# A two-layer streaming encoder step: more PSUM banks for the factors and the first heads, the queries' norm beside the heads, and another order of the final norm

## The chip, the core and the metric

The kernel runs on one core of a Trainium2 chip. The time is the device time of one execution in microseconds (us), as the median of several runs. The engines of the core are named as in the profile: PE (TensorE, the matrix products), DVE (VectorE), ACT (ScalarE), POOL (GpSimd) and SP (SyncE, which here only issues DMAs). Each engine works through its own list of instructions in order; an instruction that must wait for another engine or a DMA holds up all that stands behind it on its engine.

## What is computed

One step of a hybrid encoder for two groups of requests that share the weights: 512 tokens of a new stream and 64 of a running one, 576 columns in all, of width 1024, through two layers. Cut to what matters here:

```python
def layer(x, ...):
    x = swiglu_half(x, ffn1_norm, ffn1_w_gate, ffn1_w_up, ffn1_w_down)
    y, c_kv, k_r, wkv, shift = token_mixer(rmsnorm(x, mix_norm), ...)
    x = x + y
    x = mem_attend(x, mk, mv, lp)
    x = swiglu_half(x, ffn2_norm, ...)

def token_mixer(h, ...):
    c_q, c_kv, k_r, p_b = split(h @ w_in)                    # latents and RWKV rows
    q = (rmsnorm(c_q, q_norm) @ w_uq).reshape(b, t, 8, 96)   # 8 heads
    c_kv = rmsnorm(c_kv, kv_norm); k_r = rope(k_r, pos)
    y_a = latent attention of q over c_kv and k_r, past ones too
    kk = k * k_k * rsqrt(sum(kk * kk) + 1e-12)
    S = S * w + (S @ -kk) (kk * a) + v k;  y = S @ r         # per token, 8 heads of 64
    return concat(y_a, y_b) @ w_out, ...

y = rmsnorm(x, final_norm)                                   # after both layers
```

`rmsnorm(x, g)` is `x * rsqrt(mean(x * x) + 1e-6) * g`.

## The kernel before

The activations lie transposed in SBUF: features on the 128 partitions, the T = 576 columns as two halves of HT = 288 (`hs`). Every fp32 product is made of three products of rounded parts and remainders (lines 316 to 318, one call of `mm3`). `split` (L248 on ACT, L249 on DVE) makes the rounded part, for instance `kfh`, and the remainder, `kfl`. PSUM has eight banks, one bank per tile of a tag here.

The mixer of a layer has two stages. In the preparation two banks belong to tag `g`, four to `mm` (two tiles of two banks), one each to `sp` and `fx`. `STEPS` is the written order of its steps. `key`, `gate` and `rest` make projections in `mm`. `factors(p4)`, for four pairs of heads, spreads the keys' norm (L777, tag `sp`) and makes the lower triangles `ad` of each of the nine chunks of 64 tokens (L792 on PE, L793 on DVE, tag `fx`). They go to DRAM. `inverse(g)`, g = 0 and 1, each for two of these pairs, gathers the diagonal blocks of 16 (L814), inverts them by fifteen pairs of small DVE instructions (L818, L819), copies the result transposed (`td`, L820) and sends both to DRAM by eight DMAs (L824). `bonus` multiplies with L843 and L844. `keys` and `queries` make the latents: four of 128 features, each half 24 products into `g`, evicted by DVE L857. `rotated` makes the rotated key (`krh`, `krl`). The last step, `normed`, makes the root of the queries' norm: L361 sums the squares into an `mm` tile, and `rsqrt` (Ln, Exp, Square on ACT, L301; L350 and L351 on DVE) makes `rq`.

Then the scopes are closed and the banks given to the next stage, with tags `sc`, `tp`, `po`, `pp` of one bank and `sm` of two; `g` stays. `attention()` is a generator: for each of four pairs of heads (`pr_`) it makes values (`vp`, `vs`), keys (`kf`, `kc`) and queries (`qf`, multiplied by `rq`), each product in the next tile of `bank()`. For `pr_` 0 that goes through `g`, `g`, `sm`, `sm`, later through `g` alone. Beside it `memory(l)` makes the keys and values of the memory (`g<-x` products), and the chain goes through the nine chunks: `prepare(c)` loads `ck`, `bk` and the inverse blocks `DI` (L1090 to L1093), multiplies `bk` with `ck` (L1100, `pp`), and goes on with `batch` (L1076), the first reader of `DI`.

The final norm (`final`) is part of the last feed-forward stage. There the last four x tiles are written by halves (`some`, the add is DVE L550). `tail(a)` squares the eight x tiles of half a (ACT L1447), adds them (DVE L1449), sums over partitions (PE L1450, L1453) and takes the root. Then four outputs of two tiles each follow: two by ACT L1459 and DVE L1460, two by DVE L1463, and eight DMAs in all. `tail(0)` is called after the second x add of half 1, `tail(1)` at the end.

A scheduler sets the order of the instructions on each engine, by a timeline of its own. Who writes into a bank that another tile held before waits for that tile's last reader.

Of the kernel before, what the change touches and what calls it, by code (L numbers as in the profile page):

```python
# [11 lines left out]
AF = mybir.ActivationFunctionType  # L12
# [38 lines left out]
for _n, _c in (("ones", 128), ("eps", 4), ("id", 128), ("bd", 128), ("cen", 128), ("sel8", 32), ("sel", 128), ("mA", 256), ("mD", 64),  # L51
# [12 lines left out]
STEPS = (("decays",), ("gates",), ("key", 0), ("gate", 0), ("gate", 1), ("key", 1), ("gate", 2), ("gate", 3), ("norms", 0),  # L64
         ("key", 2), ("factors", 0), ("key", 3), ("factors", 1), ("norms", 2), ("rest", 0), ("inverse", 0), ("factors", 2),
         ("bonus", 0), ("factors", 3), ("rest", 1), ("inverse", 1), ("rest", 2), ("bonus", 1), ("rest", 3), ("bonus", 2),
         ("keys",), ("bonus", 3), ("queries",), ("rotated",), ("normed",))


def columns(op, p4=None):  # L70
# [62 lines left out]
def build(tc, I, O):  # L133
# [267 lines left out]
    def ffn(l, which, V, aside=iter(()), final=None, given=()):  # L401
# [136 lines left out]
        def last_outputs(g, acts, by_halves=None):  # L538

            w2 = [take(0 if by_halves else 2) for _ in range(2)]  # L540
            w4 = []

            def some(i, s):
                p = ps1("b")[:, 0:HT]
                for f in range(4):
                    mm3(p, cols(w4[i], f), [t[:, s] for t in acts[f]], f == 0, False)
                for f in range(2):
                    end = mm3(p, cols(w2[i // 2], i % 2 * 2 + f), [t[:, s] for t in acts[4 + f]], False, f == 1)
                o = x[4 * g + i][:, s]
                DVE.scalar_tensor_tensor(out=o, in0=p, scalar=0.5, in1=o, op0=ALU.mult, op1=ALU.add)  # L550
                return end

            for i in range(4):
                w4.append(take(0 if by_halves else (2, 2, 2, 1)[i]))
                for s in hs[0:1] if by_halves else hs:
                    some(i, s)
            if by_halves:
                for i in range(4):
                    end = some(i, hs[1])
                    if i == 1:  # L560
                        by_halves(end)


        def plain(act, ps=None, parts=(0, 1)):
# [102 lines left out]
        if final is None:  # L667
            last_outputs(1, acts)
        else:
            half_done, done = final()  # L670
            last_outputs(1, acts, half_done)
            done()
        ps.close()
        sc.close()

    def mixer(l, V, xn):
# [85 lines left out]
        def factors(p4):  # L762
# [8 lines left out]
            POOL.tensor_copy(wend[:, p4], wt[:, CH - 1::CH])  # L771
            wts.append(wt)
            kk = st([128, T], "kk")
            for s in hs:
                p = ps1("sp")
                rks[p4 // 2].to(p[:, 0:HT], p4 % 2, s)
                DVE.scalar_tensor_tensor(out=kk[:, s], in0=xk[:, s], scalar=V("kk", p4), in1=p[:, 0:HT], op0=ALU.mult, op1=ALU.mult)  # L777
            at, bk = st([128, NC, 64], "aa"), st([128, NC, 128], "big")
# [7 lines left out]

            ad = st([128, NC, 64], "ad")
            for c0, n in ((0, 5), (5, 4)):
                pa = ps1("fx")
                for c in range(c0, c0 + n):  # L790
                    for e in range(2):
                        PE.matmul(pa[half(e), (c - c0) * 64:(c - c0) * 64 + 64], bk[half(e), c, half(1)], at[half(e), c], start=True, stop=True)  # L792
                DVE.tensor_tensor(out=ad[:, c0:c0 + n], in0=pa[:, 0:64 * n].rearrange("p (c t) -> p c t", c=n),  # L793
                                  in1=C("mD").unsqueeze(1).to_broadcast([128, n, 64]), op=ALU.mult)
# [13 lines left out]
        def inverse(g):  # L808

            NP = 8 * NC  # L810
            adg, pr, tt, td = (st([128, 2, 16, 16], "x")[0:NP] for _ in range(4))
            for i in range(2):
                for e in range(2):
                    SP.dma_start(adg[36 * e:36 * e + 36, i], diagonal(ads[2 * g + i][e]))  # L814
                DVE.tensor_copy(tt[:, i], C("e16")[0:NP].rearrange("p (j s) -> p j s", j=16))
            for t in range(1, 16):
                q = pr[:, :, 0:t, 0:t]
                DVE.tensor_tensor(out=q, in0=tt[:, :, 0:t, 0:t], in1=adg[:, :, 0:t, t].unsqueeze(2).to_broadcast([NP, 2, t, t]), op=ALU.mult)  # L818
                DVE.tensor_reduce(out=tt[:, :, 0:t, t], in_=q, axis=AX.X, op=ALU.add)  # L819
            DVE.tensor_copy(td, tt.rearrange("p i j s -> p i s j"))  # L820
            for n, t_ in enumerate((td, tt)):
                for e in range(2):
                    for i in range(2):
                        SP.dma_start(diagonal(dinv[e, n, 2 * g + i]), t_[36 * e:36 * e + 36, i])  # L824
# [47 lines left out]
        for op, *n in STEPS:  # L872
# [12 lines left out]
            elif op == "queries":  # L885
                cq = [latent(nrm.rstd()) for j in range(2)]
                sqs = [squares(t) for t in cq]
                DVE.tensor_tensor(out=sqs[0], in0=sqs[0], in1=sqs[1], op=ALU.add)

                qn = []  # L890
                for j in range(2):
# [4 lines left out]
            elif op == "rotated":  # L896
                pr4 = full(C("sel"), [kr])
                krh, krl = st([128, T], "krh", F32R), st([128, T], "krl", F32R)
                split(pv(pr4), (halves(krh), halves(krl)), "kr")
                ACT.activation(out=halves(kr)[0:32], in_=pv(pr4)[0:32], func=AF.Copy)  # L900
                SP.dma_start(O["krope"][l], kr[0:32])
                cc2 = st([128, 2, PAST], "nacc")
                SP.dma_start(cc2[:, 0], I["cckv"][l])
                SP.dma_start(cc2[:, 1], I["ckrope"][l])
                cch, ccl = split(cc2, None, "cc")
                ccv = (cch[:, 0], ccl[:, 0])
            elif op == "normed":
                rq = rsqrt(pv(full(ones, sqs[0:1])), 1.0 / 256, EPS, st([128, T], "rq"), st([128, T], "rs"), halves)
        SP.dma_start(O["shift"][l], shout)
        lat.close()  # L910
        xn.close()
# [12 lines left out]
        def attention():  # L924
# [2 lines left out]

            def bank():

                tags_ = ("g", "g", "sm", "sm") if pr_ == 0 else ("g",)  # L930
                turn[0] += 1
                return ps1(tags_[(turn[0] - 1) % len(tags_)])
            kch, kcl = st([128, 2, PAST], "kch", F32R), st([128, 2, PAST], "kcl", F32R)
            for pr_ in range(4):
# [34 lines left out]
                mm3(p[:, 0:PAST], wp_[0], ccv, True, True)  # L969
                for e in range(2):  # L970
                    split(p[half(e), 0:PAST], (kch[half(e), e], kcl[half(e), e]), "kc")
                for e in range(2):
                    nr, rr = half(e), half(1 - e)
                    qf = st([128, T], "qf")
# [462 lines left out]

    def final():

        r, sq = st([128, T], "rstd"), st([128, T], "rs")  # L1440
        y = [st([128, 2, HT], "s") for _ in range(8)]

        def tail(a, prior=None):
            ss, s = ps1("b")[:, 0:HT], hs[a]
            qs = [st([128, 2, HT], "s")[:, 0] for _ in range(8)]
            for k in range(8):
# [4 lines left out]
            if prior is not None:  # L1451
                after(i, prior)
            PE.matmul(ss, ones, qs[7], start=False, stop=True)  # L1453
            rsqrt(ss, 1.0 / D, EPS, r[:, s], sq[:, s])
            for j in range(4):
                t = y[2 * j + a]
                if j < 2:
                    for i in range(2):
                        ACT.activation(out=t[:, i], in_=x[2 * j + i][:, s], func=AF.Copy, scale=V("fin", 2 * j + i))  # L1459
                    DVE.tensor_tensor(out=t, in0=t, in1=r[:, s].unsqueeze(1).to_broadcast([128, 2, HT]), op=ALU.mult)  # L1460
                else:
                    for i in range(2):
                        DVE.scalar_tensor_tensor(out=t[:, i], in0=x[2 * j + i][:, s], scalar=V("fin", 2 * j + i), in1=r[:, s], op0=ALU.mult, op1=ALU.mult)  # L1463
                SP.dma_start(O["y"][2 * j:2 * j + 2, :, s].rearrange("k p t -> p k t"), t)
        return [lambda prior=None, a=a: tail(a, prior) for a in range(2)]

    xn = open_xn()
    load_x()
# [104 lines left out]
```

## Time and profile before

| | us |
|---|---|
| median of three runs | 2796.2 |
| lowest, highest | 2794.36, 2797.31 |
| the profiled execution | 2796.16 |
| its span | 2794.4 |
| PE busy | 2740.6 |
| DVE busy | 2102.2 |
| ACT busy | 1352.5 |

The span runs from the first to the last event of the trace; some 1.8 us of the execution lie outside it. The busy time of PE counts its products also where the granted clock is halved, and so slow work counts as more. Layer 1 runs through the same program as layer 0; its hand-over from preparation to chain stands 1381.35 us later in the trace.

### The profile page before, as it was taken

How to read it: one execution, taken by the hardware profiler on the slowest of the kernel's cores; microseconds unless marked ns; L12 is line 12 of the kernel's file. 1: busy time of each engine (PE TensorE's matmuls, PEld its weight loads, DVE VectorE, ACT ScalarE, POOL GpSimd, SP SyncE). 2: the span in 40 equal slices, each digit the busy share in tenths (PEclk: the TensorE clock that was granted, in tenths of full speed). 3: DMA queues.
4: the chain of work that ended last, by engine and by line, in shares of the span. 5: the costliest groups of instructions: out<-in, count | busy, mean ns of one | idle time of the engine just before them, and what ended most of it. 6: DMA issues, size and time to landing. Idle time of an engine off the chain costs nothing.

```text
span 2794.4 us, 55844 instructions
## 1 busy us (share of the span) xinstructions
PE 2740.6 (98%) x22290; PEld 2639.7 (94%) x22290; DVE 2102.2 (75%) x4317; ACT 1352.5 (48%) x2787; POOL 86.3 (3%) x189
## 2 busy tenths in 40 slices
PE   9999999999999999999999999998999999999997
PEld 9999999888889899999999999998888899999997
DVE  8988866876677578777788778678666766887785
ACT  5554455455545544444554444544555445454443
POOL 0000001101000000000000000011010000000000
PEclk9999999989999999999999999998999999999998
DMA  5333334643333222222323222347433232232221
GB/s 194 113 115 116 104 129 117 177 117 96 106 104 121 69 92 83 91 91 91 93 75 105 91 91 91 111 117 178 116 106 118 84 111 72 84 99 91 91 84 65
DMA packets 187893, 293.47 MB, mean 105 GB/s; under 512 B 87130, under 2 KB 113370, under 8 KB 187458
## 3 DMA queue, kind: packets, MB, share of 16 engines
q1 hardware_dynamic: 185330, 285.72, 33.0%
q0 software_dynamic: 2304, 4.20, 0.6%
q8 instruction: 175, 2.87, 0.4%
q14 instruction: 84, 0.69, 0.1%
HBM read 250.63 MB, written 41.63 MB: 105 GB/s over the span
## 4 chain that ended last, share of the span: by engine, by line
PE 94%; DVE 3%; ACT 2%; DMA 1%; issue 0%; SPq 0%; DVEq 0%; ACTq 0%
PE b L318 19%; PE b L316 19%; PE b L317 18%; PE mm L316 4%; PE mm L318 4%; PE mm L317 4%; PE g L316 3%; PE g L317 3%; PE g L318 3%; PE sm L1076 2%; PE sc L316 2%; PE pp L1076 1%; PE pp L1100 1%; PE sc L317 1%; PE sc L318 1%; PE tp L1029 1%
## 5 line engine op out<-in xcount | busy, mean ns | idle before, releaser
L248 ACT ACTIVATE whi<-wraw 128x512 fp32r<-128x512 f32 (+1 forms) x497 | 308.1, 624 | 509.0 <-PE b L317 246.1
L249 DVE TENSOR_TENSOR wlo<-wraw,whi 128x512 fp32r<-128x512 f32 (+1 forms) x497 | 336.6, 680 | 114.4 <-ACT whi L248 97.5
L318 PE MATMUL b<-s,wlo 128*128 128x288 f32 x1376 | 405.4, 296 | 0.0
L317 PE MATMUL b<-s,whi 128*128 128x288 f32 x1376 | 403.0, 294 | 0.0
L316 PE MATMUL b<-s,whi 128*128 128x288 f32 x1376 | 399.4, 295 | 0.0
L316 PE MATMUL b<-xnh,whi 128*128 128x288 f32 x1128 | 332.4, 296 | 1.5 <-ACT whi L248 1.5
L317 PE MATMUL b<-xnl,whi 128*128 128x288 f32 x1128 | 332.2, 295 | 0.7 <-DVE xnl L372 0.7
L318 PE MATMUL b<-xnh,wlo 128*128 128x288 f32 x1128 | 331.3, 295 | 0.0
L317 PEld LDWEIGHTS b<-s,whi 128*128 128x128 f32 x1376 | 258.9, 188 | 0.1
L318 PEld LDWEIGHTS b<-s,wlo 128*128 128x128 f32 x1376 | 258.3, 188 | 0.0
L316 PEld LDWEIGHTS b<-s,whi 128*128 128x128 f32 x1376 | 256.4, 188 | 0.0
L318 PE MATMUL b<-s,sl 128*128 128x288 f32 x768 | 225.4, 295 | 0.0
L316 PE MATMUL b<-s,sh 128*128 128x288 f32 x768 | 224.2, 296 | 0.0
L317 PE MATMUL b<-s,sh 128*128 128x288 f32 x768 | 223.9, 292 | 0.0
L316 PEld LDWEIGHTS b<-xnh,whi 128*128 128x128 f32 x1128 | 211.9, 188 | 2.5 <-ACT whi L248 2.2
L317 PEld LDWEIGHTS b<-xnl,whi 128*128 128x128 f32 x1128 | 212.3, 188 | 1.3 <-DVE xnl L372 1.1
L318 PEld LDWEIGHTS b<-xnh,wlo 128*128 128x128 f32 x1128 | 211.7, 188 | 0.0
L318 PE MATMUL mm<-xnh,wlo 128*128 128x288 f32 x688 | 204.0, 297 | 0.0
L529 DVE SCALAR_TENSOR_TENSOR x<-b,x 128x288 f32<-128x288 f32 x320 | 140.2, 457 | 84.7 <-PE b L318 84.6
L316 PE MATMUL mm<-xnh,whi 128*128 128x288 f32 x688 | 203.8, 297 | 0.0
L317 PE MATMUL mm<-xnl,whi 128*128 128x288 f32 x688 | 203.4, 296 | 0.0
L248 ACT ACTIVATE whi<-S 128x512 fp32r<-128x512 f32 x172 | 108.5, 631 | 156.2 <-PE b L317 153.4
(511 smaller groups left out, 7351.8 us busy)
## 6 DMA issues: line engine op xcount, KB each, us to landing
wraw<-in_wgu SPq DMA_DIRECT2D x131, 512.0 KB
wraw<-in_wds SPq DMA_DIRECT2D x50, 512.0 KB
sraw<-in_wgu SPq DMA_DIRECT2D x45, 512.0 KB
wraw<-in_win SPq DMA_DIRECT2D x36, 512.0 KB
wraw<-in_wd SPq DMA_DIRECT2D x19, 512.0 KB
wraw<-in_wmk SPq DMA_DIRECT2D x16, 512.0 KB
wraw<-in_wmv SPq DMA_DIRECT2D x16, 512.0 KB
wraw<-in_wout SPq DMA_DIRECT2D x32, 256.0 KB
```

The costliest lines, as they stand in the source:

```text
L248: ACT.activation(out=h, in_=src, func=AF.Copy)
L249: by.tensor_tensor(out=lo, in0=src, in1=h.bitcast(F32), op=ALU.subtract)
L316: PE.matmul(out, wh, ah, start=first, stop=False, **kw)
L317: PE.matmul(out, wh, al, start=False, stop=False, **kw)
L318: return PE.matmul(out, wl, ah, start=False, stop=last, **kw)
L529: DVE.scalar_tensor_tensor(out=o, in0=p, scalar=0.5, in1=o, op0=ALU.mult, op1=ALU.add)
L1029: PE.transpose(pT[0:n, c0:c0 + nq], pe_[e][0:nq, kt * 128:kt * 128 + n], ident[0:nq, 0:nq])
L1076: PE.matmul(o, *f(p4, e), start=(n == 0 and p4 == 0), stop=(n == len(terms) - 1), skip_group_check=True)
L1100: i = PE.matmul(p[:, p4], bk[half(e), p4], ck[half(e), p4, 0:128], start=True, stop=True)
```

## The change

- The step `normed` goes. The queries' sums of squares are added into the tile `rq`; in `attention`, for the first pair of heads and behind the keys of the past (`kc`), two products by halves sum them over partitions in the banks `po` and `tp`, and `rsqrt` works on each half.
- `bank()` takes turns over `g`, `g`, `sm`, `sm`, `sc` for the first pair of heads.
- `factors`: the two halves of L777's spread lie in `sp` and `fx`; the two parts of L792 lie in `g` (two banks).
- `inverse`: the four DMAs of `tt` are issued ahead of the transposed copy `td`, then the copy and its four.
- The final norm: ACT's Square of the root writes a tile `s` of its own instead of `rs`, whose old readers are the last matmuls; the first half's sums come after the first x add of half 1 instead of the second. Of the first half's outputs the two that are made by DVE alone (j > 1) stand behind the last x add, and the second half's sums are written ahead of the outputs.

```diff
-         ("keys",), ("bonus", 3), ("queries",), ("rotated",), ("normed",))
+         ("keys",), ("bonus", 3), ("queries",), ("rotated",))
...
-                DVE.scalar_tensor_tensor(out=o, in0=p, scalar=0.5, in1=o, op0=ALU.mult, op1=ALU.add)
-                return end
+                return end, DVE.scalar_tensor_tensor(out=o, in0=p, scalar=0.5, in1=o, op0=ALU.mult, op1=ALU.add)
...
-                    end = some(i, hs[1])
-                    if i == 1:
+                    end, added = some(i, hs[1])
+                    if i == 0:
                         by_halves(end)
+                return added
...
-            last_outputs(1, acts, half_done)
-            done()
+            done(last_outputs(1, acts, half_done))
...
-            for s in hs:
-                p = ps1("sp")
+            for s, tag in zip(hs, ("sp", "fx")):
+                p = ps1(tag)
                 rks[p4 // 2].to(p[:, 0:HT], p4 % 2, s)
...
             for c0, n in ((0, 5), (5, 4)):
-                pa = ps1("fx")
+                pa = ps1("g")
...
-            DVE.tensor_copy(td, tt.rearrange("p i j s -> p i s j"))
-            for n, t_ in enumerate((td, tt)):
+            for n, t_ in ((1, tt), (0, td)):
+                if n == 0:
+                    DVE.tensor_copy(td, tt.rearrange("p i j s -> p i s j"))
...
-                DVE.tensor_tensor(out=sqs[0], in0=sqs[0], in1=sqs[1], op=ALU.add)
+                rq = st([128, T], "rq")
+                DVE.tensor_tensor(out=rq, in0=sqs[0], in1=sqs[1], op=ALU.add)
...
-            elif op == "normed":
-                rq = rsqrt(pv(full(ones, sqs[0:1])), 1.0 / 256, EPS, st([128, T], "rq"), st([128, T], "rs"), halves)
...
-                tags_ = ("g", "g", "sm", "sm") if pr_ == 0 else ("g",)
+                tags_ = ("g", "g", "sm", "sm", "sc") if pr_ == 0 else ("g",)
...
+                if pr_ == 0:
+
+                    pq, sq = [ps1(t)[:, 0:HT] for t in ("po", "tp")], st([128, T], "ya")
+                    for s, p in zip(hs, pq):
+                        PE.matmul(p, ones, rq[:, s], start=True, stop=True)
+                    for s, p in zip(hs, pq):
+                        rsqrt(p, 1.0 / 256, EPS, rq[:, s], sq[:, s])
...
-        r, sq = st([128, T], "rstd"), st([128, T], "rs")
+        r, sq = st([128, T], "rstd"), st([128, 2, HT], "s")
...
+        def scaled(a, j, prior=None):
...
+        def first_half(prior):
+            root(0, sums(0, prior))
+
+        def rest(last):
+            ss = sums(1)
+            for j in range(4):
+                scaled(0, j, last if j > 1 else None)
+            root(1, ss)
+            for j in range(4):
+                scaled(1, j)
+        return first_half, rest
```

The scheduler moves instructions in three places: the preparation and the hand-over of each layer, up to the chain's third chunk or so, and the end. In the lists below one row is one instruction (or as many as stand behind the x) with its line, result and operands; line numbers of the changed kernel are up to six higher in the mixer.

PE, layer 0, the first pair of heads. Before, the last product of the values, then the queries' norm in `mm`, the values and keys of the past in `sm`, the keys in `g`:

```order
L318 MATMUL g<-whi,ckvl 128x256
L361 MATMUL mm<-nsq,cst 128x288 x2
L316 MATMUL sm<-whi,cch 128x256
L317 MATMUL sm<-wlo,cch 128x256
L318 MATMUL sm<-whi,ccl 128x256
```

After, from the keys in `sc` on, with the queries' norm in `po` and `tp` and the first query of the heads behind it:

```order
L316 MATMUL sc<-ckvh,whi 128x288
L317 MATMUL sc<-ckvl,whi 128x288
L318 MATMUL sc<-ckvh,wlo 128x288
L975 MATMUL po<-rq,cst 128x288
L975 MATMUL tp<-rq,cst 128x288
L316 MATMUL sm<-qnh,whi 128x288
L317 MATMUL sm<-qnl,whi 128x288
L318 MATMUL sm<-qnh,wlo 128x288
```

The products of the norm moved behind all of the values and the first half of the keys. Further up, the last factors now stand ahead of the latents, whose eight halves of 24 products follow each other with two L843 between; further down, 51 products of the memory's keys and values stand between the heads' first products and the first reader of `DI`, where there were 26.

DVE, layer 0, the end of the second inverse (its last two steps are 72x2x14x14 and 72x2x15x15, its copy is `x<-x 72x512`). Before, it runs beside the first heads:

```order
L249 TENSOR_TENSOR kfl<-g,kfh 64x288
L249 TENSOR_TENSOR kcl<-sm,kch 64x256
L819 TENSOR_REDUCE x<-x 72x2x14
L818 TENSOR_TENSOR x<-x 72x2x15x15
L819 TENSOR_REDUCE x<-x 72x2x15
L981 TENSOR_TENSOR qf<-g,cst 64x288
L820 COPY x<-x 72x512
L982 TENSOR_TENSOR qf<-qf,rq 128x576
```

After, with the last latent's eviction (L857), the rotated key's remainder, the copy, the queries' sums of squares and their root:

```order
L817 TENSOR_TENSOR x<-x 72x2x15x15
L857 TENSOR_TENSOR lx<-g,rstd 128x288
L818 TENSOR_REDUCE x<-x 72x2x15
L249 TENSOR_TENSOR wlo<-wraw,whi 128x512
L249 TENSOR_TENSOR krl<-mm,krh 128x576
L821 COPY x<-x 72x512
L889 TENSOR_TENSOR rq<-nsq 128x576
L895 SCALAR_TENSOR_TENSOR qnl<-lx,narrow,qnh 128x576
L249 TENSOR_TENSOR wlo<-wraw,whi 128x512
L350 SCALAR_TENSOR_TENSOR ya<-po,ya 128x288
L350 SCALAR_TENSOR_TENSOR ya<-tp,ya 128x288
L351 SCALAR_TENSOR_TENSOR rq<-ya,rq 128x288 x2
```

The second inverse moved ahead, from beside the heads to between the latents' evictions, and its copy stands ahead of all that the heads read from DVE. ACT's root by halves stands ahead of its copies `vph` and `vs`, and the rotated keys (`kfh`, `kfl`, four entries) behind these.

DVE at the end of the program. Before, with the first half's root and outputs (L1460, L1463) ahead of the last x add (L550):

```order
L550 SCALAR_TENSOR_TENSOR x<-b,x 128x288 x4
L350 SCALAR_TENSOR_TENSOR rs<-b,rs 128x288
L351 SCALAR_TENSOR_TENSOR rstd<-rs,rstd 128x288
L1460 TENSOR_TENSOR s<-s,rstd 128x576 x2
L1463 SCALAR_TENSOR_TENSOR s<-x,narrow,rstd 128x288 x4
L550 SCALAR_TENSOR_TENSOR x<-b,x 128x288
L1449 TENSOR_TENSOR s<-s 128x288 x6
L350 SCALAR_TENSOR_TENSOR rs<-b,rs 128x288
```

After, where L1455 adds the squares and L1472 and L1470 make the outputs:

```order
L550 SCALAR_TENSOR_TENSOR x<-b,x 128x288 x3
L350 SCALAR_TENSOR_TENSOR s<-b,s 128x288
L351 SCALAR_TENSOR_TENSOR rstd<-s,rstd 128x288
L1455 TENSOR_TENSOR s<-s 128x288 x2
L550 SCALAR_TENSOR_TENSOR x<-b,x 128x288
L1455 TENSOR_TENSOR s<-s 128x288 x4
L550 SCALAR_TENSOR_TENSOR x<-b,x 128x288
L1472 SCALAR_TENSOR_TENSOR s<-x,narrow,rstd 128x288 x4
L1470 TENSOR_TENSOR s<-s,rstd 128x576 x2
L350 SCALAR_TENSOR_TENSOR s<-b,s 128x288
```

The six instructions of the first half's outputs moved behind the last x add, and the sums of the second half's squares between the adds. On ACT eight scaled copies (L1469) of both halves stand between the last Square of x and the Ln of the second half, where four stood.

## Rows read from the trace of the kernel before

**Rows 1.** The page, part 1: busy us (share of the span) xinstructions.
```profile
PE 2740.6 (98%) x22290; PEld 2639.7 (94%) x22290; DVE 2102.2 (75%) x4317; ACT 1352.5 (48%) x2787; POOL 86.3 (3%) x189
```

**Rows 2.** Waits of PE over the span: total us, times, longest us.
```profile
PE b L1450 <- DVE s L1449: 6.6, 1, 6.6
PE g L316 <- DVE kfl L249: 6.5, 3, 3.1
PE sm L316 <- DVE rs L350: 6.1, 2, 3.1
PE pp L1076 <- DMA DI<-d: 4.5, 2, 3.1
```

**Rows 3.** Timeline of PE, hand-over of layer 0: start, us, instruction [idle before].
```profile
547.57 0.78 PE L843 MATMUL fx<-xs,cst 128*128 128x320 f32 x2 [0.49 <-DVE x L818]
...
550.28 1.24 PE L361 MATMUL mm<-nsq,cst 128*128 128x288 f32 x4 [0.80 <-DVE nsq L888]
554.58 0.58 PE L316 MATMUL sm<-whi,cch 128*128 128x256 f32 x1 [3.06 <-DVE rs L350]
...
557.28 0.61 PE L316 MATMUL g<-ckvh,whi 128*128 128x288 f32 x1 [0.41 <-DVE vpl L249]
...
564.42 0.58 PE L316 MATMUL g<-qnh,whi 128*128 128x288 f32 x1 [3.11 <-DVE kfl L249]
...
567.57 2.07 PE L1100 MATMUL pp<-ck,bk 64*128 64x128 f32 x8
...
581.11 0.67 PE L1076 MATMUL pp<-DI,A 64*64 64x64 f32 x14 [1.32 <-DMA DI<-d]
```

**Rows 4.** Stretches: us, busy us (x) of each engine, PEclk, DMA share, GB/s.
```profile
453.60:545.20 91.60, 91.60 (x741) 84.97 (x742) 77.02 (x145) 37.36 (x62) 9.84 (x22) 1.00 0.63 151
545.20:568.70 23.50, 15.63 (x70) 13.35 (x69) 22.67 (x54) 12.34 (x24) 6.45 (x10) 0.67 0.67 213
564.00:576.00 12.00, 11.58 (x46) 10.60 (x47) 9.84 (x20) 3.05 (x6) 1.59 (x3) 0.50 0.53 92
576.00:578.00 2.00, 2.00 (x14) 2.00 (x13) 1.26 (x4) 1.29 (x4) 0.53 (x1) 0.69 0.91 232
1962.50:1967.20 4.70, 4.67 (x45) 4.23 (x46) 1.47 (x6) 1.33 (x4) 0.79 (x2) 0.64 0.33 96
```

**Rows 5.** Timeline of DVE, both inverses of layer 0.
```profile
487.91 0.16 DVE L818 TENSOR_TENSOR x<-x 72x2 f32<-72x2 f32 x1 [1.62 <-DMA x<-d]
...
542.26 0.16 DVE L818 TENSOR_TENSOR x<-x 72x2 f32<-72x2 f32 x1
...
568.12 0.60 DVE L820 COPY x<-x 72x512 f32<-72x512 f32 x1
```

**Rows 6.** Timeline of SP, the last load of DI for the first chunk of layer 0.
```profile
575.71 1.25 SPq L1093 DMA_DIRECT2D DI<-d  x2
```

**Rows 7.** Timeline of ACT, hand-over of layer 0.
```profile
551.56 0.74 ACT L301 ACTIVATE rq<-mm,cst 128x576 f32<-128x576 f32 x1 [2.10 <-PE mm L361]
...
554.73 0.68 ACT L954 ACTIVATE kfh<-krh 64x576 fp32r<-64x576 f32 x1
...
557.16 0.84 ACT L949 ACTIVATE vs<-sm 128x512 f32<-128x512 f32 x2
```

**Rows 8.** Timeline of DVE, the end.
```profile
2779.20 0.46 DVE L550 SCALAR_TENSOR_TENSOR x<-b,x 128x288 f32<-128x288 f32 x1
...
2786.70 0.46 DVE L350 SCALAR_TENSOR_TENSOR rs<-b,rs 128x288 f32<-128x288 f32 x1 [3.87 <-ACT rs L301]
```

**Rows 9.** Timeline of PE, the last two products of the last stage.
```profile
2775.89 0.29 PE L317 MATMUL b<-xnl,whi 128*128 128x288 f32 x1
2776.02 0.29 PE L318 MATMUL b<-xnh,wlo 128*128 128x288 f32 x1
```

**Rows 10.** Timeline of ACT, the end.
```profile
2780.04 1.80 ACT L1459 ACTIVATE s<-x,narrow 128x288 f32<-128x288 f32 x4
2785.22 0.50 ACT L301 ACTIVATE rstd<-b,cst 128x288 f32<-128x288 f32 x1 [3.38 <-PE b L1453]
```

More of the change, by code (lines that the diff above doesn't have):

```diff
@@ L1438, in final, with sums @@
     def final():
-        r, sq = st([128, T], "rstd"), st([128, T], "rs")
+        r, sq = st([128, T], "rstd"), st([128, 2, HT], "s")
         y = [st([128, 2, HT], "s") for _ in range(8)]
-        def tail(a, prior=None):
+        def sums(a, prior=None):
             ss, s = ps1("b")[:, 0:HT], hs[a]
@@ L1453, in tail, with root @@
             PE.matmul(ss, ones, qs[7], start=False, stop=True)
-            rsqrt(ss, 1.0 / D, EPS, r[:, s], sq[:, s])
-            for j in range(4):
[L1456 to L1465, printed above, removed]
+            return ss
+        def root(a, ss):
+            rsqrt(ss, 1.0 / D, EPS, r[:, hs[a]], sq[:, a])
+        def scaled(a, j, prior=None):
+            t, s = y[2 * j + a], hs[a]
+            if j < 2:
+                for i in range(2):
+                    ACT.activation(out=t[:, i], in_=x[2 * j + i][:, s], func=AF.Copy, scale=V("fin", 2 * j + i))
+                i = [DVE.tensor_tensor(out=t, in0=t, in1=r[:, s].unsqueeze(1).to_broadcast([128, 2, HT]), op=ALU.mult)]
+            else:
+                i = [DVE.scalar_tensor_tensor(out=t[:, i], in0=x[2 * j + i][:, s], scalar=V("fin", 2 * j + i), in1=r[:, s], op0=ALU.mult, op1=ALU.mult) for i in range(2)]
+            if prior is not None:
+                after(i[0], prior)
+            SP.dma_start(O["y"][2 * j:2 * j + 2, :, s].rearrange("k p t -> p k t"), t)
+        def first_half(prior):
+            root(0, sums(0, prior))
+        def rest(last):
+            ss = sums(1)
+            for j in range(4):
+                scaled(0, j, last if j > 1 else None)
[3 more added lines that the diff above has]
+        return first_half, rest
     xn = open_xn()
```

## The prediction

> **What bounds the kernel now.** I read the page first, then PE's waits, then the two places to which they point. PE is busy 98% of the span [rows 1], so there is little to gain: idle time of PE, work done at the lower clock, and what follows its last matmul. Of PE's waits [rows 2] the longest, 6.6 us, comes once, in the final norm. The next three are one place that comes twice, once per layer: the hand-over from the preparation of the mixer (projections, factors, latents) to the heads and the chain. There PE waits for the queries' root (3.1 us), the keys' remainders kfl (3.1) and the inverse blocks DI (1.3 in layer 0, 3.1 in layer 1).
>
> The hand-over of layer 0 is in [rows 3]: six waits, 0.49 + 0.80 + 3.06 + 0.41 + 3.11 + 1.32, in all 9.2 us of idle PE between 545 and 581. In [rows 4] it is fully busy before that, at a granted clock of 1.00, and at 0.50 (1.2 GHz) from 564 to 576. The mean of 0.67 from 545.2 to 568.7 puts the fall about 8 us in, at 553, in the idle time before 554.58; it rose between 576 and 578, in work without a gap since 564.42. Eight L1100 products take 2.07 us at that level. DVE is as full as PE there: 77.02 us busy of 91.60, then 22.67 of 23.50. So the hand-over waits for DVE's queue. What stands in that queue is the second inverse [rows 5]: thirty small instructions and a copy, from 542.26 to 568.72. Behind the copy come, on SP, eight DMAs to DRAM and the four that load DI, the last pair at 575.71 [rows 6].
>
> The profiled execution took 2796.16 us, 1.76 of them outside the span; the median is 2796.2, so differences from the span stand for both.
>
> **The banks of the factors and the order before the hand-over.** Giving L777 and L792 more banks adds no instruction. Before 545 PE has no idle time [rows 4], so the banks themselves bring PE nothing there; they let the last factors go ahead of the latents. Two things follow in the order. The second inverse's gather is issued earlier, and its instructions now stand between the latents' evictions and ahead of everything that the heads need. The first inverse can start earlier too; its start waited 1.62 us for its gather [rows 5].
>
> When does the second inverse's copy now end? From 453.6 to 568.7 DVE is busy 77.02 + 22.67 = 99.69 us and idle 15.4. About 7.2 us of this work (queries' root, one remainder of the queries, vpl, kfl, kcl, rotated queries) is now behind the copy. With no DVE idle time the copy would end at 453.6 + 99.7 − 7.2 = 546; with all of the old idle time, at 561.5. Between them I replayed the row order. The eight half-width latents now come in a row, 24 products each, 3.2 us by the 0.13 us between two neighbours of 288 columns at full clock [rows 9], and the last ends at about 546.2. DVE has 3 to 4.4 us of inverse and splits between two evictions, so it falls behind: the last eviction is done at 550.5, and its five instructions behind (2.6 us) put the end of the copy at 553. I take 553. Loading DI took 8.2 us from the copy's end (568.72) to its last pair (575.71 + 1.25 = 576.96), and PE went on at 581.11. After: about 553 + 12 = 565. Nobody asks for DI that early, so the wait of 1.3 (3.1) us goes; issuing tt's four DMAs ahead of the copy takes at most 2.6 us from a wait that is gone, and I count it at nothing.
>
> **The queries' norm beside the heads.** The same products, two half-width roots instead of one full-width: per layer two more DVE and three more ACT instructions. The old wait of 3.06 us goes: sm took over a bank in which the root's source still lay; now `po` and `tp` hold it. What is late next, in my replay: the second bank of vp waits for the last latent's eviction, 2.9 us; sm waits for the rotated key's remainder krl, 1.3; the sums of squares follow the copy (553 + 0.75), so the products `po`, `tp` end at 555.2. Then ACT works in order: before, from Ln at 551.56 to the end of vs at 558.0 it took 6.4 us [rows 7], four entries of about 0.62 us (L954) among them. Now these stand behind vs, and the six half-width entries cost about 0.8 us more than three of full width: 6.4 − 2.5 + 0.8 = 4.7. The first sm bank is free at about 559.2, a wait of 3.9 us. After that every bank's release comes before its use: the kfl that cost 3.11 us is done by 563, its reader comes at 563.5. So idle time after: 2.9 + 1.3 + 3.9 = 8.1 us, little less than 9.2, but PE runs without a gap from 559.2 and not from 564.42.
>
> **Up to the chain's first use of DI.** I let PE work at half clock from there as long as it did from 564.42 on, to about 571.5. At that level 46 products took 11.58 us [rows 4], 0.25 each, those of the memory's keys, 256 columns wide, by that 0.22; at full clock 0.13 and 0.12. From 559.2: 30 products for the heads 7.5 us, eight L1100 products 2.1, twelve of the memory's keys 2.7, to 571.5; the other twelve 1.4, L1100 at full clock 1.1, three sc and 27 more memory products 3.5: DI is used at 577.5. Against 581.11 that is 3.6 earlier, and 25 memory products more (2.9) and three sc products fewer (0.4) are done: **6.1 us in layer 0**. In layer 1 the old DI wait was longer, and the clock fell again after it: 4.7 us at 0.64 [rows 4], 1.7 us lost. In its own frame the use of DI lay 0.1 later. So 6.1 + 0.1 + 1.7: **7.9 us in layer 1**. The 25 products no longer fill the first chunks of the chain; no wait of PE of more than 0.7 us stands there now, I take 1 us off per layer (bounds 0 and 2.9).
>
> **The final norm.** Before, the last x add waited on DVE behind the first half's outputs: last matmul 2776.02 [rows 9], add at 2779.20, root at 2786.70 [rows 8]. Now those outputs stand behind it, and ACT's Square has a tile of its own, so it no longer waits for the matmuls that read the old one. The add goes at about 2776.7, the last Square ends at 2777.6, PE's sums at about 2779. On ACT eight scaled copies stand before Ln: four took 1.80 us, 0.45 each [rows 10], so Ln starts at 2777.6 + 3.6 = 2781.2 instead of 2785.22. From Ln on nothing changes: **4.0 us**. Bounds: 3 if the copies take turns with DVE's outputs, 4.5 if the first copies run before the last Square.
>
> **Sum.** 4.0 + 6.1 + 7.9 − 2.0 = 16.0 us: 2796.2 − 16.0 = **2780.2 us**. Its own range: the copy's end may lie 4 us to either side per layer, so 2772 to 2788.
>
> **The rivals.** *DVE's in-order queue becomes the bound (slower).* The second inverse stands ahead of the queries' sums on DVE and waits for its gather, and for latents that come late. Each microsecond by which the copy ends later than 553 moves po, tp, the heads and all behind by one, in both layers. For: the first inverse did wait for its gather; before, PE went on with vp and sm while the inverse ran. Against: the work ahead of the copy is 92 us in 99 us. It turns the gain into nothing at 553 + 16.0/2 = 561, all of the old idle time kept, and is slower by over 0.2% from 564 on. With the copy where it ended before, 568.7: 2796.2 − 16.0 + 31 = 2811.
>
> *The clock stays up.* The gaps are 2.9, 1.3 and 3.9 us, where 0.8 and 3.06 made it fall. Should it stay at 1.00, 12.3 us of work per layer go in half the time: 6.2 each: 2780.2 − 12.4 = 2767.8. Against: the last gap is longer than any before.
>
> *The clock falls more often.* More banks make PE go from one short group to the next and stop at each release; after DI's wait of 3.1 us in layer 1 one more fall cost 1.7 us [rows 4]. Two more per layer: 2780.2 + 6.8 = 2787. The Trainium skill, page "TensorE: Matmul & The Clock Gate", section "A second HAM failure mode: psum-queue depth-cycling", tells of a kernel in which going through the PSUM banks made PE pause so often that the clock swung between its two levels, which speaks against `bank()` with five banks. By that rule the time would be the 2787 of this rival. The trace bears it out only in part: it shows the fall after idle time of 3 us, none in the gapless stretches that use the same two g banks.
>
> *The hand-over gives nothing.* The new chain (copy, sums, root, copies on ACT, vs) ends when the old one did; kfl's wait has only changed its name. Then the tail alone is left: 2792.2. For it: idle time of 8.1 against 9.2 us is no great change; the gain hangs on its place.
>
> **Chances.** Forecast 0.55; clock up 0.14; clock falling more often 0.07; tail alone 0.17; DVE's queue 0.07. Range 2766 to 2792: the slower side and some of the clock's case are left out. About 0.2%, 5.6 us, is what a measurement of this kernel can tell from no change: faster is the forecast, both clock cases and a little of the tail's, 0.79; the same, most of the tail's case and the edge of DVE's, 0.15; slower 0.06.
>
> **What the profile after would show.** Right: the second inverse's copy at about 553 in layer 0; no wait of PE for DI; one wait for vs or the root of about 4 us; the clock back at 1.00 by about 572; in the end one x add right behind the last matmul and Ln at 4 us before its old distance from the end. Wrong: the copy beyond 560, a PE wait for kfl still at 3 us, or PE idle between 453 and 545, where there was none and where I counted the new banks and the moved inverse at nothing.

## The result, and the profile after

The changed kernel took 2781.92 us as the median of six runs (2778.92 to 2782.67) against 2795.28 of before: a ratio of 0.9947, 95% interval 0.9937 to 0.9958, that is 12 to 18 us faster. Its profiled execution took 2781.84 us, with a span of 2780.1, 14.3 less than before. Line numbers below are those of each kernel; where a line moved, the operands tell which it is (`x<-x 72x2` is the first step of an inverse, `x<-x 72x512` its copy).

To split the 14.3 us I matched instructions of the two traces with the same name and neighbours and compared their starts. The last large product came at 2766.34 us instead of 2776.02 [rows 9]: 9.7 us belong to all that is ahead of it, 4.6 to what follows. Of the 9.7, layer 0 has none: DVE's instructions of the changed kernel start 0.6 us earlier than before when the mixer of layer 0 begins and 0.2 later when it is over. All of it, 9.9 us, comes in layer 1.

PE's longest waits of the changed kernel over the span (total us, times, longest), in place of [rows 2]:

```profile
PE g L316 <- DVE lx L857: 10.4, 6, 2.8
PE sm L316 <- ACT vs L948: 6.7, 2, 3.4
PE sc L316 <- DVE kfl L249: 3.2, 2, 1.9
```

The waits for DI, for the root and the 6.6 us of the final norm are gone. In their place stand waits for the evictions of the latents (L857), for ACT's copy vs and for another kfl. The chain's first reader of DI goes on without a wait, later than before in layer 0 and earlier in layer 1; first the row of before in layer 1 (layer 0 in [rows 3]), then after in both layers:

```profile
1962.53 0.68 PE L1076 MATMUL pp<-DI,A 64*64 64x64 f32 x14 [3.14 <-DMA DI<-d]
```

```profile
581.86 0.68 PE L1082 MATMUL pp<-DI,A 64*64 64x64 f32 x16
...
1958.13 0.68 PE L1082 MATMUL pp<-DI,A 64*64 64x64 f32 x16
```

Up to there 51 (layer 0) and 53 (layer 1) products of the memory are done, where there were 26. Here is the timeline of PE in layer 0, which answers [rows 3]; the first two rows lie where PE had no idle time before:

```profile
534.14 0.40 PE L316 MATMUL g<-xnh,whi 128*128 128x288 f32 x1 [2.76 <-DVE lx L857]
...
541.63 0.37 PE L316 MATMUL g<-xnh,whi 128*128 128x288 f32 x1 [0.34 <-DVE lx L857]
...
552.00 0.39 PE L316 MATMUL g<-whi,ckvh 128*128 128x256 f32 x1 [2.25 <-DVE lx L857]
...
560.44 0.61 PE L316 MATMUL sm<-qnh,whi 128*128 128x288 f32 x1 [3.37 <-ACT vs L948]
...
566.27 0.37 PE L316 MATMUL sc<-qnh,whi 128*128 128x288 f32 x1 [1.92 <-DVE kfl L249]
567.88 0.58 PE L316 MATMUL g<-qnh,whi 128*128 128x288 f32 x1 [0.25 <-DVE kfl L249]
```

Why DVE evicts late is on DVE and SP, in place of [rows 5] and [rows 6]. First DVE, then SP's longest wait between 510 and 535 us (total us, times, longest), then its timeline, all in layer 0:

```profile
524.68 0.41 DVE L844 TENSOR_TENSOR ad<-sp,big 128x256 f32<-128x256 f32 x1
532.76 0.16 DVE L817 TENSOR_TENSOR x<-x 72x2 f32<-72x2 f32 x1 [7.67 <-DMA x<-d]
...
553.67 0.60 DVE L821 COPY x<-x 72x512 f32<-72x512 f32 x1
```

```profile
SPq L908 <- POOL narrow L705: 5.4, 1, 5.4
```

```profile
521.05 0.34 SPq L908 DMA_DIRECT2D out_shift<-narrow  x1
...
521.96 3.92 SPq L824 DMA_DIRECT2D d<-x  x4
525.92 0.47 SPq L813 DMA_DIRECT2D x<-d  x1
526.50 1.99 SPq L824 DMA_DIRECT2D d<-x  x4
528.52 1.52 SPq L813 DMA_DIRECT2D x<-d  x3
```

The second inverse's gather (L813) stands on SP between and behind the first inverse's eight writes (L824). Ahead of these stands an output, `out_shift` (L908), for which SP waits 5.4 us until POOL's copy is done; the first inverse's last step was over at 518.6 and its copy at 521.0. So the writes start at 521.96, the gather is issued at 526 to 530, and DVE, whose next instruction is the second inverse, does nothing for 7.67 us, with the latents' evictions behind it. From 532.76 to the copy DVE has no idle time of more than 0.2 us.

The clock tells the two layers apart (columns as in [rows 4]):

```profile
566.00:578.00 12.00, 11.48 (x52) 10.44 (x52) 7.36 (x14) 4.73 (x10) 0.00 (x0) 0.57 0.17 56
...
1934.00:1942.00 8.00, 4.19 (x26) 3.27 (x26) 6.47 (x13) 6.68 (x15) 1.22 (x3) 1.00 0.81 139
1942.00:1946.00 4.00, 3.20 (x16) 2.91 (x14) 1.78 (x5) 3.89 (x10) 2.00 (x5) 0.57 0.75 173
1946.00:2010.00 64.00, 61.67 (x674) 53.77 (x675) 45.46 (x118) 35.77 (x95) 3.99 (x9) 1.00 0.36 102
```

In layer 0 PE still works at a mean of 0.57 up to 578, as before. In layer 1 it is at 1.00 but for about four microseconds, where before it was at half for most of the time from 1936 to 1956 and again after the wait for DI.

The end, PE, then DVE, then ACT, in place of [rows 8 to 10]:

```profile
2766.34 0.29 PE L318 MATMUL b<-xnh,wlo 128*128 128x288 f32 x1
2766.84 0.75 PE L1456 MATMUL b<-s,cst 128*128 128x288 f32 x2 [0.20 <-DVE s L1455]
```

```profile
2766.70 0.45 DVE L550 SCALAR_TENSOR_TENSOR x<-b,x 128x288 f32<-128x288 f32 x1
2767.07 1.79 DVE L1472 SCALAR_TENSOR_TENSOR s<-x,narrow,rstd 128x288 f32<-128x288 f32 x4
...
2772.40 0.46 DVE L350 SCALAR_TENSOR_TENSOR s<-b,s 128x288 f32<-128x288 f32 x1 [2.20 <-ACT s L301]
```

```profile
2767.53 3.50 ACT L1469 ACTIVATE s<-x,narrow 128x288 f32<-128x288 f32 x8
2770.94 0.48 ACT L301 ACTIVATE rstd<-b,cst 128x288 f32<-128x288 f32 x1
```

The last x add starts 0.36 us behind the last product, where it was 3.2, and Ln starts 4.6 us behind it, where it was 9.2. The end is now ACT's eight scaled copies.

For all kernels below one table sums up the two hand-overs. Idle is the length of the stretch less PE's busy time; "at half" is PE's busy time times (1 − granted clock), summed over pieces of 2 us: the work time that the lower clock cost. Stretches: 500 to 620 us for layer 0 and 1870 to 2010 for layer 1. The last column is the lowest and highest mean granted clock over the whole span, of every run on record.

| kernel | median us | layer 0 idle | at half | layer 1 idle | at half | mean clock, all runs |
|---|---|---|---|---|---|---|
| before | 2796 | 9.7 | 9.6 | 11.0 | 9.4 | 0.987 to 0.991 |
| changed | 2781.9 | 12.1 | 8.0 | 12.1 | 1.4 | 0.993 to 0.996 |
| changed, again (e8) | 2782.1 | 11.3 | 8.8 | 11.5 | 2.7 | 0.993 to 0.995 |
| final norm alone (e1) | 2793.1 | 10.2 | 9.2 | 9.5 | 11.6 | 0.988 to 0.991 |
| banks alone (e2) | 2784.2 | 12.6 | 4.6 | 10.7 | 4.3 | 0.992 to 0.993 |
| norm and five banks alone (e3) | 2804.1 | 15.3 | 7.1 | 18.0 | 6.8 | 0.986 to 0.988 |
| changed, gather by ACT (e4) | 2768.3 | 8.3 | 0.0 | 6.4 | 4.8 | 0.996 to 0.997 |
| changed, old norm (e5) | 2778.3 | 11.6 | 5.1 | 10.3 | 4.4 | 0.993 to 0.994 |
| changed, gather by POOL (e6) | 2771.8 | 8.8 | 5.8 | 7.3 | 3.0 | 0.995 to 0.997 |
| changed, without sc (e7) | 2784.4 | 11.8 | 7.2 | 9.9 | 4.5 | 0.992 to 0.995 |
| gather by ACT, old norm (e9) | 2771.0 | 9.4 | 4.5 | 8.6 | 3.5 | 0.994 to 0.995 |
| gather by POOL, old norm (e10) | 2768.9 | 8.3 | 3.3 | 7.3 | 2.7 | 0.994 to 0.995 |

The changed kernel has more idle PE than before in both layers. What it gains ahead of the tail is work at full clock in layer 1, 8.0 us in the stretch, and 2.6 more at the end of layer 1's chain (2150 to 2215), where before the clock fell once more: 1.7 us of work at half and 0.8 of idle time. A like fall at the end of layer 0's chain, 1.7 us of work, is gone too. But both are also missing in e1 below, whose mixers have the old order, so these two can't be put down to the change. That the clock is higher after the change does not hang on one profile: in every run on record the mean clock of the changed kernel is above that of every run of before (last column), and e1, with the new end and the old mixers, lies with before.

### The profile page after: what moved, and what is told of

Its sections match the earlier page's. It is cut to its first block, busy times and chain, and to the rows that moved or that the text cites. A ratio compares the mean times of both kernels' runs of the same rounds, so it can differ in the third digit from the quotient of the medians.

```text
span 2780.1 us, 55881 instructions
## 1 busy us (share of the span) xinstructions
PE 2726.5 (98%) x22290; PEld 2627.9 (95%) x22290; DVE 2098.3 (75%) x4321; ACT 1352.2 (49%) x2793; POOL 104.6 (4%) x189
## 4 chain that ended last, share of the span: by engine, by line
PE 93%; DVE 3%; ACT 2%; DMA 1%; issue 1%; SPq 0%; DVEq 0%; ACTq 0%
PE b L318 19%; PE b L316 19%; PE b L317 19%; PE mm L316 4%; PE mm L317 4%; PE mm L318 4%; PE g L316 3%; PE g L317 3%; PE g L318 3%; PE sm L1082 2%; PE sc L316 2%; PE pp L1082 2%; PE sc L318 1%; PE pp L1106 1%; PE sc L317 1%; PE tp L1035 1%
```

## Experiments

Ratios are to runs of the kernel before on the same chip (medians there 2796.3, 2795.9 and 2796.3 us in the three groups).

**The final norm alone (e1).** Before, with the hunks of `final` and `last_outputs`.

```diff
-            last_outputs(1, acts, half_done)
-            done()
+            done(last_outputs(1, acts, half_done))
```

> The kernel before with the new final norm alone (x add, Square tile, outputs behind the last add). Theory: the order of everything ahead of the last stage is unchanged, and the end gives what the profile after shows there, 4.6 us from the last large product to the end of the span (18.4 before, 13.8 after). So about 2790.7 us against 2795.3, and the hand-overs of both layers with the same waits as before (kfl 3.1, rs 3.1, DI 1.3 and 3.1). Rival: a part of the 4.6 us is the clock or chance; then the time lies above 2792.5.

Measured: 2793.09 us, ratio 0.9991 (0.9982 to 1.0), eleven runs from 2787.5 to 2798.3. In its profile the last large product starts at 2774.00 and the span ends at 2787.7: 13.7 us, as in the changed kernel, against 18.4. So the end is shorter by what the theory says. The median shows 3 us and lies on the rival's side of 2792.5; that this is scatter is likely, since the runs of this program spread over 11 us, but not shown. Ahead of the tail, where the order is the same, its profile is 2.0 us shorter than that of before (2774.00 against 2776.02), and the clock differs at the ends of the two chains. Before, then e1:

```profile
794.00:802.00 8.00, 7.26 (x43) 6.57 (x43) 5.66 (x10) 5.27 (x10) 0.00 (x0) 0.79 0.16 43
2182.00:2190.00 8.00, 6.83 (x38) 6.60 (x39) 6.46 (x11) 6.30 (x12) 0.00 (x0) 0.79 0.13 37
```

```profile
794.00:802.00 8.00, 7.25 (x56) 6.71 (x56) 6.09 (x11) 6.62 (x12) 0.00 (x0) 1.00 0.25 75
2182.00:2190.00 8.00, 7.12 (x51) 6.66 (x51) 7.01 (x12) 4.88 (x9) 0.00 (x0) 1.00 0.13 35
```

So a fall there comes or does not come with one and the same order, and the table's columns of the hand-overs differ by up to 2.2 us between these two profiles.

**The factors' banks alone (e2).** Before, with these lines.

```diff
-            for s in hs:
-                p = ps1("sp")
+            for s, tag in zip(hs, ("sp", "fx")):
+                p = ps1(tag)
...
-                pa = ps1("fx")
+                pa = ps1("g")
```

> The kernel before with the factors' banks alone (spread in sp and fx, L792 in g); queries' norm and final norm as before. Theory: the banks alone move the second inverse ahead of the latents' evictions; its gather stands on SP behind the first inverse's writes, so DVE waits about 7.7 us for it and PE about 5 us per layer for L857; DI comes early, no wait for DI (1.3 and 3.1 before); sm still waits for the queries' root, now behind the copy. Gain 3 to 7 us: 2788 to 2792. Rival (the norm's place is what gives, the banks nothing or a loss): 2794 to 2799.

Measured: 2784.16 us, ratio 0.9962 (0.995 to 0.9975), 7 to 14 us faster, more than the theory's upper end. The order did what it said: no wait for DI, and waits for L857. The root's wait stays, 3.05 us; PE's timeline in layer 0:

```profile
552.75 0.39 PE L316 MATMUL g<-whi,ckvh 128*128 128x256 f32 x1 [1.70 <-DVE lx L857]
555.80 2.26 PE L361 MATMUL mm<-nsq,cst 128*128 128x288 f32 x4 [2.08 <-DVE nsq L888]
561.11 0.58 PE L316 MATMUL sm<-whi,cch 128*128 128x256 f32 x1 [3.05 <-DVE rs L350]
```

Its idle time in both layers is no less than before's (23.3 against 20.7); half of the loss at the low clock is gone (table), and so are the falls at the chains' ends. The td copy's order is the old one here, and DI is not waited for: the turned order of the inverse's DMAs is not needed for that.

**The queries' norm and the five banks alone (e3).** Before, with the hunks on `normed`, `rq` and `bank`.

```diff
-                tags_ = ("g", "g", "sm", "sm") if pr_ == 0 else ("g",)
+                tags_ = ("g", "g", "sm", "sm", "sc") if pr_ == 0 else ("g",)
...
+                    for s, p in zip(hs, pq):
+                        PE.matmul(p, ones, rq[:, s], start=True, stop=True)
+                    for s, p in zip(hs, pq):
+                        rsqrt(p, 1.0 / 256, EPS, rq[:, s], sq[:, s])
```

> The kernel before with the queries' norm beside the heads and five banks for the first heads alone; factors' banks and final norm as before. Theory: the second inverse stays beside the heads and its copy comes even later, so DI is the bound: the wait of 3.06 us for the root goes and the wait for DI grows by about as much (from 1.3 and 3.1 to 3 to 7): within 3 us of before, 2792 to 2798. Rival (the norm gives the gain of layer 1): 2784 to 2789.

Measured: 2804.1 us, ratio 1.0033 (1.002 to 1.0046): slower by 6 to 13 us, beyond both theories. Without the banks the second inverse stays beside the heads, and DVE and ACT now have the heads' splits, the inverse and the root in one list. PE waits longer for all of them, and for DI as before:

```profile
561.11 0.58 PE L316 MATMUL sc<-qnh,whi 128*128 128x288 f32 x1 [5.22 <-DVE kfl L249]
568.41 2.07 PE L1106 MATMUL pp<-ck,bk 64*128 64x128 f32 x8 [2.08 <-DVE A L1109]
...
576.53 0.53 PE L316 MATMUL sc<-kfh,qh 128*128 128x192 f32 x1 [3.95 <-ACT pexp L301]
...
586.77 0.68 PE L1082 MATMUL pp<-DI,A 64*64 64x64 f32 x14 [1.22 <-DMA DI<-d]
```

DI is used at 586.8 instead of 581.1. The theory named DI as the bound that would take the gain; by these waits DVE's list was it, ahead of DI. The norm and the fifth bank change together here, so which of the two costs is not told.

**The gather off SP's queue (e4, e6).** The changed kernel with one line other:

```diff
-                    SP.dma_start(adg[36 * e:36 * e + 36, i], diagonal(ads[2 * g + i][e]))
+                    (ACT if g else SP).dma_start(adg[36 * e:36 * e + 36, i], diagonal(ads[2 * g + i][e]))
```

In e6 `POOL` stands for `ACT`.

> The changed kernel with the second inverse's four gathers issued from ACT's queue instead of SP's, where they stood behind the first inverse's writes. Theory: DVE's wait of 7.7 us for the gather was the reason that it fell behind the latents; without it the second inverse starts at about 525 instead of 532.8 in layer 0 and PE's waits for L857 (5.3 and 5.0 us per layer) go: 2770 to 2775, unless the clock takes some of it. Rival (the gather was covered, DVE's load in sum decides): PE's waits move to vs and kfl, 2779 to 2783.

> The changed kernel with the second inverse's gathers issued from POOL's queue. Other than with ACT's queue, ACT's and DVE's order around the queries' root stays that of the changed kernel. Theory (the gather's place in SP's queue costs, about 7.7 us of DVE per layer): DVE's wait for the gather falls to 4 us or less, PE's waits for L857 fall from 5 to under 1.5 us per layer, time 2768 to 2776, the wait for vs of 3.4 us stays. Rival (the gain with ACT's queue came from the root that there stands behind vs and the keys on ACT): 2779 to 2783.

Measured: 2768.3 us with ACT, ratio 0.9902 (0.9889 to 0.9916), and 2771.77 with POOL, 0.9906 (0.9893 to 0.992); both are 10 us and more faster than the changed kernel, with ACT even below the theory's 2770. DVE's wait falls from 7.67 to 2.83 and 2.94 us, here with ACT:

```profile
528.47 0.16 DVE L817 TENSOR_TENSOR x<-x 72x2 f32<-72x2 f32 x1 [2.83 <-DMA x<-d]
```

PE's waits for L857 fall to 1.1 us in all with ACT and to 0.3 in layer 0 with POOL, and the second inverse's copy ends 3 to 4 us earlier than at 554.3, here with ACT, then with POOL:

```profile
550.50 0.59 DVE L821 COPY x<-x 72x512 f32<-72x512 f32 x1
```

```profile
549.52 0.62 DVE L821 COPY x<-x 72x512 f32<-72x512 f32 x1
```

With ACT's queue the order of ACT's list changed too (the root stands behind vs), but in layer 0 with POOL it did not, and PE still waits for what stands behind the root there, now vpl instead of vs:

```profile
555.17 0.37 PE L316 MATMUL g<-ckvh,whi 128*128 128x288 f32 x1 [3.87 <-DVE vpl L249]
```

So the rival, that the gain came from ACT's order, falls: the gather's place on SP cost the changed kernel about 10 us. The scheduler also sets the latents' evictions and the inverse's steps in another order on DVE when the gather comes early; what that alone is worth, and whether `out_shift` or the eight writes held the gather, no run tells. The price of ACT's queue shows on ACT: the four issues go out over 6.24 us, and a copy that has to follow DVE's L713, done at 520.5, stands behind them until 523.89. First the issues, with the shortest, median and longest in ns, then L713 on DVE, then ACT:

```profile
L813 ACTq DMA_DIRECT2D x<-d x4: 297/300/579, 517.6 to 523.5; - x4
```

```profile
519.69 0.80 DVE L713 SCALAR_TENSOR_TENSOR big<-shp,narrow,big 128x576 f32<-128x576 f32 x1
```

```profile
517.61 6.24 ACTq L813 DMA_DIRECT2D x<-d  x4
523.89 0.39 ACT L714 ACTIVATE big<-shp,narrow 128x1 f32<-128x1 f32 x1 [5.51 <-DMA d<-x]
```

The issues themselves take some 1.5 us of the 6.24; the rest is waiting between them, and the trace gives the end of the copy's wait to a DMA.

**The norm's old place, everything else changed (e5, e9, e10).** The hunks on `normed` and `rq` taken back, with the gather on SP (e5), ACT (e9) and POOL (e10).

> The changed kernel with the queries' norm back where it was before (whole width, in a tile of mm, at the end of the preparation); banks, five banks for the heads, inverse's DMAs and final norm stay changed. Theory: once the banks have moved the second inverse ahead, the norm's place is worth nothing: banks alone gave 2784.2, the final norm 4.6, so 2777 to 2783. Rival (the norm beside the heads saves the wait of 3.06 us per layer for the root, as the prediction had it): 2786 to 2791.

> The gathers of the second inverse on ACT's queue and the queries' norm back where it was before; banks and final norm stay changed. Theory: the two are independent; the norm's old place was worth 3.8 us with the late gather, and in the run with ACT's queue alone the root stood behind vs on ACT and cost less: 2763 to 2768. Rival (with the second inverse early the wait of 3.06 us for the root counts again, as the prediction had it): 2770 to 2776.

> The same with the gathers on POOL's queue. Theory: the same 3.8 us against the run with POOL's queue alone (2771.8): 2766 to 2770; PE's wait for vpl (3.9 us per layer there, behind ACT's root) goes, a wait of about 3 us for the root in mm comes. Rival: 2772 to 2776.

Measured: 2778.31 us (ratio 0.9934, 0.9921 to 0.9946) with SP, as the theory had it, 3.8 less by the median than the changed kernel beside it (e8, 2780.1 to 2782.8; here 2777.1 to 2780.2, so the runs of the two just touch). 2770.97 (0.9913, 0.9898 to 0.9928) with ACT, 2.7 more than e4, as the rival had it, though the intervals overlap. 2768.92 (0.9907, 0.9891 to 0.9924) with POOL, by the median 2.9 less than e6, by the ratio (0.9906) no different. So the norm's move brings nothing once the banks have moved the inverse: by the medians it costs some 4 us in the changed kernel, and with the gather early it is worth 3 us or less to either side. That the two are independent, the theory behind e9, is not borne out. The traces suggest that the root's place on ACT decides (ahead of vs in the changed kernel and e6, behind it in e4); no run changes that place alone, so this is not shown.

**Four banks (e7) and the changed kernel again (e8).**

```diff
-                tags_ = ("g", "g", "sm", "sm", "sc") if pr_ == 0 else ("g",)
+                tags_ = ("g", "g", "sm", "sm") if pr_ == 0 else ("g",)
```

> The changed kernel with four banks in turn for the first heads, g, g, sm, sm, without sc. Theory: the fifth bank lets two more products of the heads go ahead of a release; without it PE waits about 1 to 2 us longer per layer for kfl or vs: 2783 to 2787. Rival (by then PE waits for DVE's and ACT's lists, not for a bank): 2780 to 2783.

> The changed kernel once more, on the chip of the three others. Theory: where PE's clock falls in a hand-over is not set by the order alone; the two layers need not again be 8.0 and 1.4 us of work lost at half clock as in the first profile, while the waits of PE (5.3, 3.4, 1.9 in layer 0) stay within 0.3 us. Time 2778 to 2784. Rival (the program sets it): the same two losses within 1 us.

Measured: 2784.43 us without `sc` (2779.3 to 2785.9) beside 2782.09 (2780.1 to 2782.8) for the changed kernel. The medians lie as the theory said, the runs overlap: the fifth bank is worth some 2 us, no more. The waits moved: instead of vs it is vpl (3.9 us per layer) and then qf.

The repeated run has the time of the first and its waits within 0.7 us, where 0.3 was expected (L857 4.6 in layer 0, vs 3.4, kfl 1.8). Its low clock costs 8.8 and 2.7 us where it was 8.0 and 1.4, layer 0 much and layer 1 little again. My theory that these sums would change from run to run is not borne out, though the rival's limit of 1 us is missed by 0.3. The falls themselves did move: from 534 to 540 the clock is 0.72 in the second profile and 1.00 in the first, from 552 to 560 it is 0.97 and 0.78. What differs between the layers I can't say: their order and waits are alike.

## Why the prediction was right, and where it was not

**Right on the wait for DI and on the end.** The second inverse's copy ended at 554.3 (553 was forecast), DI was loaded long before its use and no wait for it is left, and the wait for the second bank of vp (2.25 for 2.9) and the wait for vs (3.37 for 3.9) came where the replay put them; the 1.3 us for krl did not come in layer 0. That e2 alone takes the wait for DI away, and e3 without the banks does not, shows that the banks' effect on the order does it, as the prediction said; and e2 alone is 7 to 14 us faster, so the banks carry most of the gain. The final norm gave 4.6 for 4.0: the last add came 0.36 us behind the last product and the eight copies took 3.50, both a little less than counted.

**The second inverse's gather was counted at nothing.** The prediction read that the first inverse waited 1.62 us for its gather and set the old idle time of DVE as the bound, but it did not follow SP's list: the gather stood behind `out_shift` and the first inverse's writes. DVE waited 7.67 us, PE 2.76 and 0.34 in a stretch in which the prediction counted no idle time and named such idle time as a sign of being wrong. This is the mechanism of its first rival, DVE's list held up by the gather. That the copy still ended near the forecast 553 is luck. The forecast stands 7 us behind its bound without idle time, 546; from 453.6 to the copy's end DVE is in fact busy 89.2 of 100.7 us, so idle for 11.5, 7.67 of them at the gather, and has some 3 us less work ahead of the copy than the prediction counted. With the gather early the copy ends at 551.1 (e4) and 550.1 (e6). Taken away, it is worth another 10 to 14 us by the medians (e6, e4).

**"Every bank's release comes before its use" was wrong.** The replay let `sc` go free with the first of its two remainders kfl and put it at 563. The second came at 565.67, behind ACT's four copies of the rotated key, and PE waited 1.92 us for it. So PE did not run without a gap from 559.2 on.

**The clock was sized wrong in both layers.** Twelve microseconds at half per layer were forecast, a loss of 6.2. Layer 0 lost 8.0, most of it behind the late gap (0.57 from 566 to 578, where 1.00 was forecast from 572 on); layer 1 lost 1.4. The terms of 6.1 and 7.9 us, with 1 off each, should have given 5 in layer 0 and 7 in layer 1; they gave −0.8 and 9.9. The forecast use of DI, 577.5 in layer 0, came at 581.86, 0.75 us later than before; in layer 1 it came 4.4 us earlier than before. The sum, 9.1 or 9.7 with the start's 0.6, is near the forecast 12, but its parts are not: layer 1 was close to the rival in which the clock stays up, layer 0 to the rival in which the hand-over gives nothing. And both parts count the end of a chain, where before a fall cost 1.7 us of work that e1 saves with the old order. So that the total came out within 2 us is in part luck.

**The norm's move was taken for a gain.** The wait of 3.06 us for the root went, as forecast, and vs behind the root on ACT came in its place with 3.37. The prediction saw that wait and still took the place for a gain, because it counted on work without a gap behind it. With the old place the kernel is 3.8 us faster by the medians (e5).

**The rule weighed in the prediction.** In the first profile with five banks the clock fell three times in layer 0, where before it fell once, and once in layer 1, where it fell three times; over both hand-overs that is four falls before, four and three in the two profiles with five banks, and three without `sc`. Without `sc` it lost 11.7 us of work at half in the two layers, with it 9.4 and 11.5. By that rule the time would have been 2787; neither the time nor these counts bear it out.

## What to carry to other kernels

When a change lets work go ahead on one engine, follow each DMA that it needs through the list of the queue that issues it: a load that stands behind an output and the stores of the step before goes out when these have gone (7.67 us of DVE here), and an engine that waits for the load holds up all that it evicts. A bank is free when the last of its readers is done, so count all of them. And a sum that comes out does not show that its parts were right: compare each term with the trace, layer by layer. The run with the least idle time (e4) had the best time, though its loss at the low clock went from 0 to 4.8 us between its layers.

The fastest version measured is the changed kernel with the gathers on ACT's queue, 2768.3 us (2763.7 to 2769.8), 28 us under the kernel before; with POOL's queue and the norm's old place it is 2768.9 (2767.4 to 2771.1), no different.

## What the runs showed of the hardware that I had not expected

After a wait of 2.25 us for the same eviction the clock fell in layer 0 (0.78 from 552 to 560) and did not fall in layer 1, where the wait was 2.24 (1.00 from 1934 to 1942), with the same instructions around. In the second profile of the same kernel (e8) layer 0's falls lay elsewhere: 0.97 from 552 to 560, after a wait of 1.60 us, but 0.72 from 534 to 540, after one of 3.02, where the first profile shows 1.00 after one of 2.76. A layer's loss at half clock went from 0 (layer 0 of e4, with gaps of up to 2.88 us) to 11.6 us (layer 1 of e1).

Eleven runs of one program (e1) spread over 11 us, while the changed kernel's spread over 4. In the changed kernel the time goes with the mean granted clock (0.996 in the fastest run, 0.993 in the slowest of its six); in e1 it does not (0.989 in the fastest and in the slowest), so what spreads those runs stays open.
